# FFN-in of a hybrid layer by a block scheme of seven products, with weight sums partly by accumulating DMAs

## The chip, the core and the metric

The kernel runs on one core of one Trainium2 chip. The metric is the device time of one execution in microseconds (us): 807.37 us, the median of three runs (807.11 to 808.28).

## What is computed

One layer of a decoder trunk: 512 tokens, model width 1024, all in float32. A mixer of three parts (short convolution, stick-breaking attention, a chunked scan) is merged by gates and projected by w_o; then comes a gated FFN of width 2816. Each sub-layer is scaled and shifted by rows that a conditioning vector c gives through mod_w.

```python
mod = jax.nn.silu(c) @ mod_w + mod_b
shift1, scale1, gate1, shift2, scale2, gate2 = split(mod, 6)
...
merged = sigmoid(gl_a) * y_a + sigmoid(gl_b) * y_b + sigmoid(gl_c) * y_c
mix_out = merged @ w_o
x = x + gate1 * rms_norm(mix_out, g_post_mix)

h2 = rms_norm(x, g_pre_ffn) * (1 + scale2) + shift2
gt, up = jnp.split(h2 @ w_ffn_in, 2, axis=-1)
f = (jax.nn.silu(gt) * up) @ w_ffn_out
return x + gate2 * rms_norm(f, g_post_ffn)
```

## The kernel before

**Products in parts.** Each float32 operand is split into a high part (a cast to float32r) and a low part (the rest); a product is three matmuls into one PSUM bank: high by high, high by low, low by high (mm3, L150 to L153). split (L146 to L148) makes the parts: ACT casts (L147), DVE subtracts (L148).

**Weights.** SP loads each weight chunk into one of three raw buffers of 128x2048 (raw_tile, L74). split_piece takes 1024 columns of it and makes a piece, whi and wlo, in one of four buffers each. piece() (L212) hands out the next piece and lets the splits run three pieces ahead (LOOK). All chunks stand in one list in the order of use, the columns of mod_w for the modulation rows between them.

**Order.** The start is scheduled by hand (L316). From there a scheduler puts the instructions of PE, DVE, ACT and POOL in an order and each engine runs its own list in order. PSUM has eight banks that are handed out in turn.

**Modulation rows.** mods_in_turn (L894) is a side job that is pumped along beside the attention, the gates and FFN-out. A step covers 256 columns: mod_acc multiplies and adds the eight row groups of a mod_w chunk on DVE (L230 once, L232 seven times), L906 adds the bias, which POOL loads (L903), and two matmuls with ones spread the row over the partitions. Some steps lie beside the attention, whose own chain on DVE and POOL is sb_e (L591), the mask (L573, POOL), sb_hi (L596) and sb_lo (L597), and on PE the matmul pz (L625).

**Merge and w_o.** The three gated branches are multiplied and added on DVE (L954 and the next lines) and split. w_o runs in two pairs of 128-token blocks; after each block x1_chain (L975) norms, adds the residual and makes two tiles xm (L996), and h2_tiles (L1000) transposes them (L1004) and splits the result into h2h and h2l (L1007, L1008).

**FFN-in.** 22 column blocks of 128 for the gate and 22 for the up half, k = 1024 in eight steps, three matmuls each. The first two blocks of each half run on tokens 0 to 255 first, because the last two xm are not ready then, and on tokens 256 to 511 after; the other 20 pairs run 512 tokens wide (ffn_mm, L1030; L1040 to L1056). Behind each pair, ACT makes the sigmoid and DVE two products (L1060, L1061), and split makes fh and fl.

**FFN-out.** For each half of the output columns, all blocks of f by w_ffn_out, 512 wide, into a bank for each 128 tokens (L1070 to L1121).

Of the kernel before, what the change touches and what calls it, by code (L numbers as in the profile page):

```python
# [7 lines left out]
F32 = mybir.dt.float32  # L8
# [24 lines left out]
def hybrid_block(ctx: ExitStack, tc, x, c, mod_w, mod_b, g_pre_mix, g_post_mix, g_pre_ffn,  # L33
# [112 lines left out]
    def split(hi, lo, src):  # L146
        act.copy(hi, src)  # L147
        vec.tensor_tensor(lo, src, hi.bitcast(F32), ALU.subtract)  # L148
# [26 lines left out]
    def load_chunk():  # L175
        kind, groups, ncol, npc = chunks[at["dma"]]
        at["dma"] += 1
        got = []
        for parts in groups:
            raw = raw_tile()[:, 0:KD * 256 if kind != "cols" else KD * ncol]  # L180
            raw = raw.rearrange("p (k n) -> p k n", n=ncol)
            for k0, nk, src in parts:
                pat = "(p k) n -> p k n" if kind == "mod" else "(k p) n -> p k n"
                nc.sync.dma_start(raw[:, k0:k0 + nk, :], src.rearrange(pat, k=nk))
            got.append(raw)
        if kind == "mod":
            raws.append(got[0])
        for j in range(npc):
            for raw in got:
                pieces.append((kind, raw, ncol, j))  # L190

    def split_piece():
        while at["split"] >= len(pieces):
            load_chunk()
        kind, raw, ncol, j = pieces[at["split"]]
        n = {"cols": P, "v": 264, "rows": ncol}[kind]
        nk = {"cols": KD, "v": 2, "rows": 1024 // n}[kind]
# [14 lines left out]
    def piece():  # L212

        i = at["use"]
        at["use"] += 1
        while at["split"] < min(i + LOOK, n_pieces):
            with tc.high_priority() if at["split"] < 5 else nullcontext():
                split_piece()
        return pieces[i]

    def mod_chunk():
# [6 lines left out]
    def mod_acc(acc, mw):  # L228

        vec.tensor_scalar(acc, mw[:, 0], sc8[:, 0:1], None, op0=ALU.mult)  # L230
        for r in range(1, KD):
            vec.scalar_tensor_tensor(acc, mw[:, r], sc8[:, r:r + 1], acc, op0=ALU.mult,  # L232
                                     op1=ALU.add)

# [217 lines left out]

    def w_mod(part, q4):
        n0 = part * D + q4 * 256
        chunks.append(("mod", [[(0, KD, mod_w[:, n0:n0 + 256])]], 256, 0))
# [21 lines left out]
    for _ in range(2):  # L477
        for kp in range(4):
            w_rows(w_o, 2 * kp, 2, slice(0, D), D)
    for mp in range(MF // 2):  # L480
        chunks.append(("cols", [[(0, KD, w_ffn_in[:, o + mp * 256:o + (mp + 1) * 256])]
                                for o in (0, FFN)], 256, 2))
    for hf in range(2):
        for k0 in range(0, MF, 4):
            w_rows(w_ffn_out, k0, min(4, MF - k0), half(hf), 512)
            if hf == 0 and k0 // 4 < 4:
                w_mod(5, k0 // 4)
    n_pieces = sum(ch[3] * len(ch[1]) for ch in chunks)
# [404 lines left out]

    def mods_in_turn(steps, rest):  # L894

        def sums(part, q4):
            dsts, gain, plus = rows_of[part]
            n0 = part * D + q4 * 256
            if gain is not None and q4 % 2 == 0:
                nc.gpsimd.dma_start(dsts[q4 // 2],  # L900
                                    gain[0, q4 * 256:q4 * 256 + 512].partition_broadcast(P))
            brow = sm.tile([1, 256], F32, tag="brow", name="brow", bufs=2)
            nc.gpsimd.dma_start(brow, mod_b[n0:n0 + 256].unsqueeze(0))  # L903
            acc = sm.tile([P, 256], F32, tag="macc", name="macc2")
            mod_acc(acc, mod_chunk())
            vec.tensor_tensor(acc[0:1, :], acc[0:1, :], brow, ALU.add)  # L906
            am = sm.tile([P, 2, 256], FR, tag="mah", name="mah", bufs=1)
            split(am[:, 0, :], am[:, 1, :], acc)
            return am

        def row(part, q4, am):
            dsts, gain, plus = rows_of[part]
            dst = dsts[q4 // 2][:, (q4 % 2) * 256:(q4 % 2) * 256 + 256]
            pm = bank("pmr")
            pe.matmul(pm[:, 0:256], onesr, am[:, 0, :], start=True, stop=False)
            pe.matmul(pm[:, 0:256], onesr, am[:, 1, :], start=False, stop=True)
            if gain is None:
                act.copy(dst, pm[:, 0:256])
            else:
                vec.scalar_tensor_tensor(dst, pm[:, 0:256], plus, dst, op0=ALU.add,  # L920
                                         op1=ALU.mult)
        last = None
        for n, st_ in enumerate(steps):
            if last is not None:
                row(*last)
            last = st_ + (sums(*st_),)
            yield
            if rest and n % 2:
                yield
        yield  # L930
        row(*last)


    mh, ml = [], []
    sides.append(mods_in_turn(mods, True))
    for mp in range(4):
# [6 lines left out]
        for j in range(2):  # L943
# [3 lines left out]
            for b, (k0, nk, bh, bl) in enumerate(((0, 2, yah, yal), (2, 2, ybh, ybl),  # L947
# [6 lines left out]
                vec.tensor_tensor(gt, gt, pb, ALU.mult)  # L954
                if b:
                    vec.tensor_tensor(gt, gt, acc, ALU.add)
                acc = gt
            mh.append(t2("mh", FR))
            ml.append(t2("ml", FR))
            split(mh[m], ml[m], acc)  # L960
        gts = nxt


    h2h = gp.tile([P, KD, T], FR, tag="h_hi", name="h2h")
    h2l = gp.tile([P, KD, T], FR, tag="h_lo", name="h2l")
    x1 = gp.tile([P, NTB, D], F32, tag="x16", name="x1")
# [32 lines left out]

    def h2_tiles(tb, xms):  # L1000
        for q in range(2):
            pt = bank("pt2")
            for j in range(4):
                pe.transpose(pt[:, blk(j)], xms[q][:, blk(j)], ident)  # L1004
            p3 = pt.rearrange("p (k t) -> p k t", k=4)
            dst = slice(4 * q, 4 * q + 4)
            act.copy(h2h[:, dst, blk(tb)], p3)  # L1007
            vec.tensor_tensor(h2l[:, dst, blk(tb)], p3, h2h[:, dst, blk(tb)].bitcast(F32),  # L1008
                              ALU.subtract)

# [18 lines left out]

    def ffn_mm(pt, w, ts, first, last):  # L1030
        for k in range(KD):
            mm3(pt[:, ts], w[0][:, k, :], w[1][:, k, :], h2h[:, k, ts], h2l[:, k, ts], k == 0,
                k == KD - 1)

    lo_t, hi_t, all_t = slice(0, 256), slice(256, 512), slice(0, 512)
    pf = {}
    fw = {}
    for i in range(4):
        pf[i], fw[i] = bank("pf"), piece()
        ffn_mm(pf[i], fw[i], lo_t, True, False)  # L1040
        if i == 2:
            h2_tiles(*todo.pop(0))
    h2_tiles(*todo.pop(0))
    ma.close()
    fp = ctx.enter_context(tc.tile_pool(name="fp", bufs=1))
    fq = ctx.enter_context(tc.tile_pool(name="fq", bufs=2))
    fh = fp.tile([P, MF, T], FR, name="fh")
    fl = fp.tile([P, MF, T], FR, name="fl")
    for i in range(4):
        ffn_mm(pf[i], fw[i], hi_t, False, True)  # L1050
    for m in range(MF):
        if m < 2:
            pg, pu = pf[2 * m], pf[2 * m + 1]
        else:
            pg, pu = bank("pfg"), bank("pfu")
            for pt in (pg, pu):  # L1056
                ffn_mm(pt, piece(), all_t, True, True)
        f = fq.tile([P, T], F32, tag="f", name="f")
        sigm(f, pg)
        vec.tensor_tensor(f, f, pg, ALU.mult)  # L1060
        vec.tensor_tensor(f, f, pu, ALU.mult)  # L1061
        split(fh[:, m, :], fl[:, m, :], f)

# [6 lines left out]
    def fo_mm(o, tb, w, k0, cs):  # L1070
        for k in range(2):
            mm3(o[:, cs], fh[:, k0 + k, blk(tb)], fl[:, k0 + k, blk(tb)], w[0][:, k, cs],
                w[1][:, k, cs], k0 + k == 0, k0 + k == MF - 1)

    NPF = MF // 2
    for hf in range(2):
# [5 lines left out]
        for i in range(NPF - LATE):  # L1082
            w = piece()
            for tb, acc, cs in groups:
                fo_mm(acc, tb, w, 2 * i, cs)
            if hf == 0:
                if i == 0:
                    sides.append(mods_in_turn([(5, q4) for q4 in range(4)], False))
                pump()
        for i in range(NPF - LATE, NPF):  # L1090
            ws[i] = piece()
        for tb, acc, cs in groups:
            for i in range(NPF - LATE, NPF):
# [55 lines left out]
```

## Time and profile before

| what | value |
|---|---|
| median of three runs | 807.37 us (807.11 to 808.28) |
| the profiled execution | 807.41 us |
| its span in the profile | 805.7 us |
| FFN-in on PE (first start to the first of FFN-out) | 429.2 to 675.7 us |
| FFN-out on PE | from 675.7 us |
| mean granted clock | 0.997 |

The profile is one execution. Its span goes from the first to the last instruction; the execution's own time has 1.7 us more around it. PE is the matmul engine and PEld its weight loads, DVE, ACT, POOL and SP are the others, and a q behind a name means its DMA queue. L with a number is a line of the kernel. In rows of the timeline stand the start, the duration, the engine and line, the operation with output and input, shapes, and in brackets the idle time before it and what ended it.

### The profile page before, as it was taken

Reading aid. Unit: us, or ns where it says so; the run is one execution under the profiler, and the core shown is the slowest. Engines: PE = TensorE matmul, PEld = TensorE weight load, DVE = VectorE, ACT = ScalarE, POOL = GpSimd, SP = SyncE. Lnnn points to the kernel's source line nnn. Section 1 sums busy time; section 2 is a strip of 40 time slices with the busy share of each in tenths; the row PEclk is TensorE's granted clock in tenths of the full one; section 3 lists DMA queues with packets and bytes.
Section 4 is the critical chain, followed back from the end, with each engine's and each line's share of the span. In section 5 each row is a group of like instructions: output and inputs, shape, how many; then the busy total and the mean of one; then the engine's idle time right before and its main releaser. Section 6 shows DMA issues by size and latency. Waiting matters only on the chain.

```text
span 805.7 us, 9651 instructions
## 1 busy us (share of the span) xinstructions
PE 775.2 (96%) x3677; PEld 634.2 (79%) x3677; DVE 495.5 (62%) x783; ACT 373.2 (46%) x625; POOL 122.5 (15%) x169
## 2 busy tenths in 40 slices
PE   3899999999899999999999999999999999999997
PEld 2679887767578888888878988888888888888886
DVE  5999968568967968748498544334344357423214
ACT  5566544565667445463465534434334433213112
POOL 4453412345421000000033000000000000000000
PEclk9999999999999999999999999999999999999999
DMA  9981441120534566452754322322333345532102
GB/s 281 297 258 58 130 131 53 53 85 31 184 121 154 187 201 206 129 173 101 262 169 145 102 84 78 103 81 79 102 105 104 105 148 195 170 115 96 35 1 105
DMA packets 96959, 105.07 MB, mean 130 GB/s; under 512 B 3276, under 2 KB 86272, under 8 KB 96912
## 3 DMA queue, kind: packets, MB, share of 16 engines
q1 hardware_dynamic: 94320, 99.62, 38.6%
q0 software_dynamic: 1824, 3.75, 1.6%
q10 hardware_dynamic: 768, 1.07, 0.4%
q8 instruction: 29, 0.48, 0.2%
q14 instruction: 18, 0.15, 0.1%
HBM read 102.33 MB, written 2.10 MB: 130 GB/s over the span
## 4 chain that ended last, share of the span: by engine, by line
PE 83%; DVE 11%; DMA 2%; issue 2%; ACT 1%; POOL 1%; DVEq 0%; POOLq 0%
PE pgt L151 5%; PE pgt L153 5%; PE pgt L152 5%; PE pfg L152 5%; PE pfu L152 5%; PE pfu L151 5%; PE pfg L151 5%; PE pfu L153 4%; PE pfg L153 4%; PE pfo L152 4%; PE pfo L153 4%; PE pfo L151 4%; DVE smacc L254 2%; PE pbr L151 2%; PE pbr L152 2%; PE pbr L153 2%
## 5 line engine op out<-in xcount | busy, mean ns | idle before, releaser
L147 ACT CAST whi<-wraw 128x1024 fp32r<-128x1024 f32 (+1 forms) x133 | 137.7, 1035 | 303.4 <-PE pfg L152 77.5
L148 DVE TENSOR_TENSOR wlo<-wraw,whi 128x1024 fp32r<-128x1024 f32 (+1 forms) x133 | 164.4, 1236 | 152.8 <-ACT whi L147 148.0
L151 PE MATMUL pgt<-hh,whi 128*128 128x512 f32 x192 | 75.7, 394 | 0.0
L153 PE MATMUL pgt<-hh,wlo 128*128 128x512 f32 x192 | 75.4, 393 | 0.0
L152 PE MATMUL pgt<-hl,whi 128*128 128x512 f32 x192 | 75.4, 393 | 0.0
L152 PE MATMUL pfu<-h2l,whi 128*128 128x512 f32 x160 | 63.0, 394 | 0.0
L152 PE MATMUL pfg<-h2l,whi 128*128 128x512 f32 x160 | 63.0, 394 | 0.0
L151 PE MATMUL pfu<-h2h,whi 128*128 128x512 f32 x160 | 62.7, 392 | 0.0
L151 PE MATMUL pfg<-h2h,whi 128*128 128x512 f32 x160 | 62.7, 392 | 0.0
L153 PE MATMUL pfu<-h2h,wlo 128*128 128x512 f32 x160 | 62.1, 388 | 0.0
L153 PE MATMUL pfg<-h2h,wlo 128*128 128x512 f32 x160 | 62.1, 388 | 0.0
L153 PE MATMUL pfo<-whi,fl 128*128 128x512 f32 x154 | 60.9, 395 | 0.0
L152 PE MATMUL pfo<-wlo,fh 128*128 128x512 f32 x154 | 60.9, 395 | 0.0
L151 PE MATMUL pfo<-whi,fh 128*128 128x512 f32 x154 | 60.8, 395 | 0.0
L903 POOL DMA_DIRECT2D brow<-in_mod_b_dram x16 | 8.1, 504 | 332.0 <-DVE macc L906 331.4
L232 DVE SCALAR_TENSOR_TENSOR macc<-wraw,sc,macc 128x256 f32<-128x256 f32 x112 | 55.8, 499 | 3.2
L153 PEld LDWEIGHTS pgt<-hh,wlo 128*128 128x128 f32 x192 | 36.1, 188 | 8.2
L151 PEld LDWEIGHTS pgt<-hh,whi 128*128 128x128 f32 x192 | 36.1, 188 | 7.8 <-issue 0.4
L152 PEld LDWEIGHTS pgt<-hl,whi 128*128 128x128 f32 x192 | 36.1, 188 | 7.5
L1061 DVE TENSOR_TENSOR f<-f,pfu 128x512 f32<-128x512 f32 x20 | 13.8, 688 | 40.3 <-PE pfu L153 40.3
L151 PEld LDWEIGHTS pfu<-h2h,whi 128*128 128x128 f32 x160 | 30.0, 188 | 7.0
L151 PEld LDWEIGHTS pfg<-h2h,whi 128*128 128x128 f32 x160 | 30.0, 188 | 7.0
(360 smaller groups left out, 1701.5 us busy)
## 6 DMA issues: line engine op xcount, KB each, us to landing
wraw<-in_w_ffn_in_dram SPq DMA_DIRECT2D x22, 1024.0 KB, 5.1
wraw<-in_w_in_dram SPq DMA_DIRECT2D x20, 1024.0 KB, 5.3
wraw<-in_mod_w_dram SPq DMA_DIRECT2D x16, 1024.0 KB, 5.4
wraw<-in_w_ffn_out_dram SPq DMA_DIRECT2D x10, 1024.0 KB, 5.0
wraw<-in_mod_w_dram SPq DMA_DIRECT2D x16, 512.0 KB, 6.1
wraw<-in_w_o_dram SPq DMA_DIRECT2D x8, 1024.0 KB, 4.9
xn<-in_x_dram SPq DMA_DIRECT2D x8, 256.0 KB, 5.7
wraw<-in_w_ssm_out_dram SPq DMA_DIRECT2D x4, 512.0 KB, 7.0
```

Source lines behind the costliest of these rows:

```text
L147: act.copy(hi, src)
L148: vec.tensor_tensor(lo, src, hi.bitcast(F32), ALU.subtract)
L151: pe.matmul(o, whi, xhi, start=start, stop=False)
L152: pe.matmul(o, whi, xlo, start=False, stop=False)
L153: pe.matmul(o, wlo, xhi, start=False, stop=stop)
L232: vec.scalar_tensor_tensor(acc, mw[:, r], sc8[:, r:r + 1], acc, op0=ALU.mult, op1=ALU.add)
L254: vec.scalar_tensor_tensor(acc[:, r % 2, :], mw2[:, r], sc8[:, r:r + 1], acc[:, r % 2, :], op0=ALU.mult, op1=ALU.add)
L903: nc.gpsimd.dma_start(brow, mod_b[n0:n0 + 256].unsqueeze(0))
L1061: vec.tensor_tensor(f, f, pu, ALU.mult)
```

## The change

**The scheme.** FFN-in is computed by unit: two column blocks (0 and 1) of both the gate and the up half, so 11 units. The k range is halved, the tokens are halved. In place of eight block products there are seven per unit; each (product, numbered 1 to 7) is 24 matmuls: gate and up, four k steps, three parts, 256 tokens wide. Four take plain weights, and three (5, 6 and 3) take sums of weights. On the other side, products take sums of the token halves.

**Weight sums.** For a unit, wino_load loads 1 MB per column block in two halves with rows of 512 bytes; every fourth goes into a new, fourth raw buffer. DVE adds the two k halves of block 1 (wsum, L262). POOL issues a DMA that adds block 0 into block 1 in SBUF (L263, 512 KB), and, after the splits of pieces 5 and 6, DMAs that add block 0's halves to wsum (L270, 512 KB each). That makes three such adds per unit.

**Activation sums and results.** For the second token half, DVE and ACT make the sums and split them (L1147 to L1168), before product 5. The PSUM results are combined on DVE (L1196 to L1236). The first two units run side by side, with products 1 and 2 on the first token half first. f stays in float32 (f4s); its split is moved into FFN-out (f_split).

**Modulation rows and merge.** A modulation step now covers 512 columns in two chunks of four row groups; the first row is scaled on ACT (L965), the seven others are added on DVE (L967), and the bias is added by an accumulating DMA. The sums of the merge are accumulating DMAs but for the last block (L1014), and a merged block is split one block later.

The diff, cut to its core:

```diff
+    NU = MF // 2
+    WINO = [(u, q) for q in (1, 2, 5, 6, 7, 4, 3) for u in range(2)]
+    WINO += [(u, q) for u in range(2, NU) for q in (5, 1, 4, 6, 7, 2, 3)]
...
+    def wino_load(u, i):
+        at["wino"] = at.get("wino", 0) + 1
+        if at["wino"] % 4:
+            raw = raw_tile()
+        else:
+            raw = late_pool["fx"].tile([P, 2048], F32, tag="raw4", name="wraw", bufs=1)
...
+            nc.sync.dma_start(raw[:, g], w_ffn_in[:, c0:c0 + P].rearrange(
+                "(k p) n -> p k n", k=8))
...
+        if q == 5:
...
+            vec.tensor_tensor(un["s"], un[1][0], un[1][1], ALU.add)
+            nc.gpsimd.dma_start(un[1][0], un[0][0], accum_op=ALU.add)
+        src = {1: (0, 0), 2: (0, 1), 4: (1, 1), 7: (1, 0)}.get(q)
+        src = un[src[0]][src[1]] if src else un["s"]
...
+        split(hi, lo, src)
+        if q in (5, 6):
+            nc.gpsimd.dma_start(un["s"], un[0][q - 5], accum_op=ALU.add)
...
-    mods = [(p_, q4) for p_ in (2, 3, 4) for q4 in range(4)]
+    mods = [(p_, hf, rh) for p_ in (2, 3, 4) for hf in range(2) for rh in range(2)]
...
+            for rh in range(2):
+                mw = mod_chunk()
+                for r in range(4):
+                    c_ = sc8[:, 4 * rh + r:4 * rh + r + 1]
+                    if rh + r == 0:
+                        act.activation(acc, mw[:, r], AF.Copy, scale=c_)
+                    else:
+                        vec.scalar_tensor_tensor(acc, mw[:, r], c_, acc, op0=ALU.mult,
+                                                 op1=ALU.add)
...
+            nc.gpsimd.dma_start(acc[0:1, :], mod_b[n0:n0 + 512].unsqueeze(0), accum_op=ALU.add)
...
+                elif m < 7:
+                    nc.gpsimd.dma_start(acc, gt, accum_op=ALU.add)
...
+                for part, (a_, b_) in enumerate(((hi, xh), (hi, xl), (lo, xh))):
+                    pe.matmul(o[:, cs], a_[:, g, k, :], b_,
+                              start=(start and g + k + part == 0),
+                              stop=(stop and k == 3 and part == 2), skip_group_check=True)
...
+        vec.tensor_tensor(t1_, hbh[:, 0, :, t0].bitcast(F32), p12, ALU.subtract)
+        vec.tensor_tensor(t1_, t1_, hbl[:, 0, :, t0].bitcast(F32), ALU.add)
+        split(hbh[:, 3, :, t0], hbl[:, 3, :, t0], t1_)
...
+    for u in range(2, NU):
+        p5 = bank("pf5")
+        product(5, p5, True, True)
+        pa1, u2 = bank("pfa"), u2_tile()
+        product(1, pa1, True, True)
+        act.copy(u2, pa1)
+        p4 = bank("pf4")
+        product(4, p4, True, True)
+        p6 = bank("pf6")
+        product(6, p6, True, True)
+        vec.tensor_tensor(u2, p6, u2, ALU.add)
+        p7 = bank("pf7")
+        product(7, p7, True, True)
...
+        vec.tensor_tensor(c2[:, 0, :], p7, u2, ALU.add)
+        vec.scalar_tensor_tensor(c2[:, 1, :], p5, -1.0, c2[:, 0, :], op0=ALU.mult,
+                                 op1=ALU.subtract)
+        vec.tensor_tensor(c2[:, 0, :], p4, c2[:, 0, :], ALU.subtract)
+        gated_m1(u, c2)
+        product(2, pa1, False, True)
+        gated_m0(u, pa1, 0)
+        product(3, p5, False, True)
+        vec.tensor_tensor(u2, p5, u2, ALU.add)
+        gated_m0(u, u2, 1)
...
+    with tc.high_priority():
+        f_split(0)
+        f_split(1)
```

**How the order moves.** At the start of FFN-in, DVE before, from the last xm (the tiles that PE transposes) on; wlo are low parts of weights, pt2 the transposed tiles, f the gated result:

```order
L996 SCALAR_TENSOR_TENSOR xm_3880<-xm_3880,st_3868,SH_2233 128x512
L996 SCALAR_TENSOR_TENSOR xm_3886<-xm_3886,st_3868,SH_2234 128x512
L1008 TENSOR_TENSOR h2l_3477<-pt2_4027,h2h_3476 128x4x128
L1008 TENSOR_TENSOR h2l_3477<-pt2_4034,h2h_3476 128x4x128
L148 TENSOR_TENSOR wlo_3957<-wraw_3952,whi_3956 128x1024
L1060 TENSOR_TENSOR f_4146<-f_4146,pf_3893 128x512
```

The same place after, first piece; u2, sg and c2 hold sums of the activations, txh, txl, hbh and hbl their parts:

```order
L1058 SCALAR_TENSOR_TENSOR xm_3765<-xm_3765,st_3753,SH_2233 128x512
L1058 SCALAR_TENSOR_TENSOR xm_3771<-xm_3771,st_3753,SH_2234 128x512
L262 TENSOR_TENSOR wsum_3928<-wraw_3678 128x1024
L1156 TENSOR_TENSOR u2_3938<-hbh_3356,pt2_3866 128x512
L1162 TENSOR_TENSOR u2_3940<-sg_3939,pt2_3866 128x512
L148 TENSOR_TENSOR wlo_3932<-wsum_3928,whi_3931 128x1024
L1157 TENSOR_TENSOR u2_3938<-u2_3938,hbl_3357 128x512
L148 TENSOR_TENSOR txl_3937<-u2_3940,txh_3936 128x4x128
L1160 SCALAR_TENSOR_TENSOR c2_3941<-u2_3938,sg_3939 128x512
L148 TENSOR_TENSOR hbl_3357<-u2_3938,hbh_3356 128x4x128
L1164 TENSOR_TENSOR c2_3941<-hbh_3356,c2_3941 128x512
L148 TENSOR_TENSOR txl_3937<-c2_3941,txh_3936 128x4x128
```

Six rows on (left out here: L1165, hbl, L1156, txl, L1157, L1162), the second piece, up to the weights of product 5 of unit 1:

```order
L1160 SCALAR_TENSOR_TENSOR c2_3962<-u2_3959,sg_3960 128x512
L148 TENSOR_TENSOR hbl_3357<-u2_3959,hbh_3356 128x4x128
L148 TENSOR_TENSOR txl_3937<-u2_3961,txh_3936 128x4x128
L148 TENSOR_TENSOR txl_3937<-c2_3962,txh_3936 128x4x128
L1164 TENSOR_TENSOR c2_3962<-hbh_3356,c2_3962 128x512
L148 TENSOR_TENSOR hbl_3357<-sg_3960,hbh_3356 128x4x128
L1165 TENSOR_TENSOR c2_3962<-c2_3962,hbl_3357 128x512
L262 TENSOR_TENSOR wsum_3998<-wraw_3995 128x1024
L148 TENSOR_TENSOR txl_3937<-c2_3962,txh_3936 128x4x128
L1172 TENSOR_TENSOR f4_3914<-sg_3980,pfa_3778 128x256
L1173 TENSOR_TENSOR f4_3914<-f4_3914,pfa_3778 128x256
L148 TENSOR_TENSOR wlo_4002<-wsum_3998,whi_4001 128x1024
```

Where two subtractions (h2l) followed the last xm, the activation sums and two weight sums with their low parts follow now.

At the start of FFN-out, DVE before; macc2 is a modulation step, the matmuls of FFN-out begin with blocks whose fl lies far ahead of these rows:

```order
L148 TENSOR_TENSOR wlo_5532<-wraw_5529,whi_5531 128x1024
L1060 TENSOR_TENSOR f_5512<-f_5512,pfg_5452 128x512
L1061 TENSOR_TENSOR f_5512<-f_5512,pfu_5453 128x512
L230 TENSOR_SCALAR macc2_5661<-wraw_5662,sc8_132 128x256
L148 TENSOR_TENSOR wlo_5576<-wraw_5529,whi_5575 128x1024
L148 TENSOR_TENSOR fl_4049<-f_5512,fh_4048 128x512
```

After, from the last combination (L1234, which reads product 3) on; fparts with f4_3914 is the first unit's low part of f:

```order
L1234 TENSOR_TENSOR u2_6276<-pf5_6246,u2_6276 128x512
L1173 TENSOR_TENSOR f4_3924<-f4_3924,c2_6395 128x512
L148 TENSOR_TENSOR wlo_6538<-wraw_6497,whi_6537 128x1024
L1172 TENSOR_TENSOR f4_3924<-sg_6435,pfa_6275 128x256
L967 SCALAR_TENSOR_TENSOR macc2_6532<-wraw_6569,sc8_132,macc2_6532 128x512
L1173 TENSOR_TENSOR f4_3924<-f4_3924,pfa_6275 128x256
L967 SCALAR_TENSOR_TENSOR macc2_6532<-wraw_6569,sc8_132,macc2_6532 128x512
L1172 TENSOR_TENSOR f4_3924<-sg_6470,u2_6276 128x256
L967 SCALAR_TENSOR_TENSOR macc2_6532<-wraw_6569,sc8_132,macc2_6532 128x512
L1173 TENSOR_TENSOR f4_3924<-f4_3924,u2_6276 128x256
L148 TENSOR_TENSOR fparts_6481<-f4_3914,fparts_6480 128x1024
```

The low part that FFN-out needs first has moved from the stage before to the end of this list.

More of the change, by code (lines that the diff above doesn't have):

```diff
@@ L892, in hybrid_block, with mods_in_turn, row @@
     rows_of = {2: (G1, g_post_mix, 0.0), 3: (SH, None, 0.0), 4: (SC, g_pre_ffn, 1.0)}
-    def mods_in_turn(steps, rest):
-        def sums(part, q4):
+    def mods_in_turn(steps, rest, parts_):
+        def row(part, hf, am):
             dsts, gain, plus = rows_of[part]
[L898 to L913, printed above, removed]
+            dst = dsts[hf]
@@ L927, in mods_in_turn @@
             yield
-            if rest and n % 2:
+            am = parts_()
+            split(*am, acc)
+            last = (part, hf, am)
+            if rest:
                 yield
@@ L1027, in hybrid_block @@
             todo.append((tb, x1_chain(tb, pos[tb])))
[L1030 to L1042, printed above, removed]
@@ L1043, in hybrid_block @@
-    h2_tiles(*todo.pop(0))
-    ma.close()
[L1045 to L1062, printed above, removed]
+    lo_t, hi_t = slice(0, 256), slice(256, 512)
```

236 lines of the change are left out of this document (193 added, 43 removed).

## The prediction

> **What bounds the kernel now.** I read the page's first part and its chain, then PE's waits by stage, then the busy time of each engine in the FFN-in stage, then single rows of DVE and PE where the change puts work in PE's way. The page's engine row and chain row:
>
> ```profile
> PE 775.2 (96%) x3677; PEld 634.2 (79%) x3677; DVE 495.5 (62%) x783; ACT 373.2 (46%) x625; POOL 122.5 (15%) x169
> PE 83%; DVE 11%; DMA 2%; issue 2%; ACT 1%; POOL 1%; DVEq 0%; POOLq 0%
> ```
>
> PE is busy for 96% of the span and carries 83% of the chain. Where it waits at all from 180 us on, the waits view names three places (total, times, longest):
>
> ```profile
> PE pz L625 <- DVE sb_hi L596: 1.9, 1, 1.9
> PE pz L625 <- DVE sb_lo L597: 1.2, 1, 1.2
> PE pt L1004 <- DVE xm L996: 2.5, 2, 1.4
> ```
>
> The first two lie in the stick-breaking attention, the third at the border of w_o and FFN-in. Inside FFN-in nothing waits; the windows view from 480 to 680 us (busy PE, PEld, DVE, ACT, POOL, clock, DMA share, GB/s):
>
> ```profile
> 480.00:680.00 200.00, 200.00 (x875) 164.02 (x874) 89.37 (x113) 80.81 (x109) 2.13 (x4) 1.00 0.33 108
> ```
>
> So a matmul less there is time off the end, if DVE (45% busy), ACT (40%) and the DMAs can feed the shorter stage, and if PE starts and ends it as promptly as before.
>
> **Term 1, matmuls.** PE's timeline, the first and the last of 72 matmuls of 256 columns in a row, then the first and last starts of the 512-wide FFN-in and of FFN-out by tile:
>
> ```profile
> 429.22 0.28 PE L151 MATMUL pf<-h2h,whi 128*128 128x256 f32 x1
> 437.58 0.28 PE L153 MATMUL pf<-h2h,wlo 128*128 128x256 f32 x1
> L151 PE MATMUL pfg<-h2h,whi x160: 392/392/392, 456.0 to 669.5; 128*128 128x512 f32 x160
> L151 PE MATMUL pfo<-whi,fh x154: 392/394/398, 675.7 to 794.9; 128*128 128x512 f32 x154
> ```
>
> A 256-wide matmul takes 8.36/71 = 0.1177 us; 960 wide ones took 675.7 - 456.0 = 219.7 us, 0.2288 each. FFN-in was 192 x 0.1177 + 219.7 = 242.3 us. The change issues 11 units x 7 products x 24 = 1848 matmuls of 256 columns: 217.6 us. Term: -24.7. Only seven eighths of the multiplications are left, and the narrow form gives 3% of that back. The Trainium skill, "TensorE: Matmul & The Clock Gate", Part 1: The HAM clock gate, has back-to-back matmuls at N/2.4 GHz plus about 2.5 ns. By it they would be 109 and 216 ns (estimate from that page) and the term -26.3; the rows are 6 to 8% slower, and the rows decide.
>
> **Term 2, the start of FFN-in (seam 1).** The four products on the first token half come first as before. Before, PE then needed the last xm, eight transposes and one copy. DVE's xm and PE around it:
>
> ```profile
> 442.17 1.41 DVE L996 SCALAR_TENSOR_TENSOR xm<-xm,st,SH 128x512 f32<-128x512 f32 x2
> 441.28 0.28 PE L153 MATMUL pf<-h2h,wlo 128*128 128x256 f32 x1
> 442.98 1.32 PE L1004 MATMUL pt<-ident,xm 128*128 128x128 f32 x8 [1.42 <-DVE xm L996]
> 444.31 0.74 PE L151 MATMUL pf<-h2h,whi 128*128 128x256 f32 x4
> 445.04 0.39 PE L152 MATMUL pf<-h2l,whi 128*128 128x256 f32 x1
> ```
>
> Four matmuls before 445.04 at full pace is 444.6, PE's restart free of stalls. Now the order has 18 DVE instructions after those xm before the last low part that product 5 reads (L148 hbl<-u2_3959, itself the eighteenth): two of 1024 columns, two scalar_tensor_tensor of 512, fourteen others of 512. Their start-to-start from DVE's timeline, with two 256-wide rows for later:
>
> ```profile
> 413.02 1.22 DVE L148 TENSOR_TENSOR wlo<-wraw,whi 128x1024 fp32r<-128x1024 f32 x1
> 414.15 0.69 DVE L988 TENSOR_TENSOR x<-x,t2k 128x512 f32<-128x512 f32 x1
> 414.75 0.69 DVE L1008 TENSOR_TENSOR h2l<-pt,h2h 128x512 fp32r<-128x512 f32 x1
> 415.36 0.74 DVE L986 SCALAR_TENSOR_TENSOR t2k<-pwo,st,G 128x512 f32<-128x512 f32 x1
> 416.01 0.68 DVE L1008 TENSOR_TENSOR h2l<-pt,h2h 128x512 fp32r<-128x512 f32 x1
> 205.81 0.42 DVE L779 TENSOR_TENSOR ce<-ce,xs 128x256 f32<-128x256 f32 x1
> 206.14 0.69 DVE L815 TENSOR_TENSOR ys<-ys,sgz 128x512 f32<-128x512 f32 x1
> ```
>
> That is 1.13 for 1024 columns, 0.605 for 512, 0.65 for scalar_tensor_tensor, 0.33 for 256. So 2 x 1.13 + 2 x 0.65 + 14 x 0.605 = 12.0; DVE is free of xm at 443.5, PE restarts at T = 455.5, 10.9 later than 444.6. Nothing else is ready for PE then. Behind T, ten more DVE instructions up to wlo_4002, which product 5 of unit 1 reads (six of 512 columns, two of 256, two of 1024: 6 x 0.605 + 2 x 0.33 + 2 x 1.13), end at T + 6.5, while product 5 of unit 0 lasts 2.8, so PE waits again. Then the POOL add of unit 1 (L270) goes out, and product 6 of unit 1 needs it landed, cast and subtracted. No accumulating DMA is in this trace. The nearest rows: POOL's own loads, a 1 KB one, and the weights (KB each, median us to landing); with them the group rows of the cast and of four POOL issues:
>
> ```profile
> x<-in_x_dram POOLq DMA_DIRECT2D x4, 512.0 KB, 5.2
> SC<-in_g_pre_ffn_dram POOLq DMA_DIRECT2D x2, 256.0 KB, 7.1
> G<-in_g_post_mix_dram POOLq DMA_DIRECT2D x2, 256.0 KB, 3.5
> wraw<-in_w_ffn_in_dram SPq DMA_DIRECT2D x22, 1024.0 KB, 5.1
> wraw<-in_mod_w_dram SPq DMA_DIRECT2D x16, 512.0 KB, 6.1
> wraw<-in_mod_w_dram SPq DMA_DIRECT2D x16, 1024.0 KB, 5.4
> L147 ACT CAST whi<-wraw 128x1024 fp32r<-128x1024 f32 (+1 forms) x133 | 137.7, 1035 | 303.4 <-PE pfg L152 77.5
> L968 POOL DMA_DIRECT2D x<-in_x_dram x4 | 2.1, 538 | 37.8 <-PE pbr L153 37.8
> ```
>
> I take A = 5.2 us for an add of 512 KB, the POOL row of the same size, and keep 3.5 and 7.1 as ends. Product 6 of unit 1 can start at T + 6.5 + 0.5 (issue) + 5.2 + 1.04 + 1.13 = T + 14.4; without waits it would start three products (8.5) after T. That is 5.9 more, and 10.9 + 5.9 = 16.8. Term: +16.8 (15.1 to 18.7).
>
> By the Trainium skill, "Collectives: The Full Stack", The bandwidth ceiling: the fold count and why AG ≠ RS ≠ AR, an add in a DMA reads two sources for one write, so twice the reading of a copy. An estimate by that page is an add that lasts as much longer than a plain load as 512 KB more would, 6 to 7 us, and a forecast some 1.5 us higher; no run shown has such a transfer, and the sum stays with the rows.
>
> **Term 3, the start of FFN-out (seam 2).** Before, fl of the last block was not needed first, and no wait is listed there. Now the first split of f (f_split(0)) stands on DVE behind all of the last unit: after PE's end of product 3, L1234, L1173 of 512, a wlo, four 256-wide, three L967, and the split itself: 0.6 + 0.6 + 1.13 + 4 x 0.33 + 3 x 0.65 + 1.13 = 6.7. Two matmuls (0.46) need only the high part, so PE stands for 6.3. After such idling the clock is low; windows around the attention's two waits (clock is the third number from the end):
>
> ```profile
> 212.00:214.00 2.00, 0.50 (x1) 0.19 (x1) 1.81 (x4) 0.34 (x1) 0.49 (x2) 1.00 0.00 0
> 214.00:216.00 2.00, 1.44 (x5) 0.91 (x7) 2.00 (x6) 0.00 (x0) 0.00 (x0) 0.60 0.00 0
> 216.00:218.00 2.00, 2.00 (x14) 1.36 (x16) 1.67 (x3) 1.97 (x4) 1.30 (x2) 0.55 0.78 250
> 218.00:220.00 2.00, 2.00 (x16) 1.39 (x13) 1.08 (x2) 0.81 (x3) 1.76 (x2) 1.00 1.07 362
> ```
>
> Four us at 0.575 after 3.1 us of waiting lose 1.7. Term: +6.3 + 1.7 = +8.0 (6.3 to 9). In seam 1 the same loss falls into the wait until T + 6.5 and costs nothing.
>
> **Term 4, the attention's waits.** DVE's rows ahead of them, and SP's two loads of modulation weights:
>
> ```profile
> 206.74 1.12 DVE L230 TENSOR_SCALAR macc<-wraw,sc 128x256 f32<-128x256 f32 x1
> 207.89 3.21 DVE L232 SCALAR_TENSOR_TENSOR macc<-wraw,sc,macc 128x256 f32<-128x256 f32 x5
> 212.28 0.49 DVE L596 CAST sb_hi<-sb_e 128x512 fp32r<-128x512 f32 x1 [0.19 <-POOL sb_e L573]
> 212.69 1.21 DVE L148 TENSOR_TENSOR wlo<-wraw,whi 128x1024 fp32r<-128x1024 f32 x1
> 213.82 0.68 DVE L597 TENSOR_TENSOR sb_lo<-sb_e,sb_hi 128x512 fp32r<-128x512 f32 x1
> 177.73 22.03 SPq L184 DMA_DIRECT2D wraw<-in_mod_w_dram  x2
> ```
>
> The new steps put 1.3 us of L967 and a wlo there in place of 4.3 us of L230 and L232, and sb_lo follows sb_hi at once. If that were all, both waits (3.1) and most of the clock loss (1.7) would go. But L967 now also stands in front of the sb_hi of the step before, and reads the second half chunk, whose load could go out only at 177.73 + 22.03 = 199.8. With 5.4 us it lands at 205.2, up to 1.3 sooner as the first half needs less of DVE. From there 0.65 + 0.33 + 0.65 + 0.6 to that sb_lo, 5.3 of work up to the next sb_e, then 0.6, 0.7 for the mask, 0.33 and 0.6 end sb_lo at 213.6 to 214.9, where 214.5 was. I take -0.3, and half of the clock loss, -0.9. Term: -1.2 (-4.5 to +4).
>
> **What costs nothing, and its cover.** Steady units last 168 x 0.1177 = 19.8 us. DVE has 8 x 1.13 + 6 x 0.6 + 0.65 + 4 x 0.33 = 14.6 in each, so it keeps up. The adds and loads form a loop: in an even unit, a load L, two POOL issues, an add, cast and subtract, an issue and an add (2A + L + 3.7), since POOL has the next unit's L263 ahead of L270; in an odd one two loads, two issues and an add (A + 2L + 1). Together 3(A + L) + 4.7 must stay under 39.6, so A + L under 11.6. With 5.2 and 5.1 it does. The accumulating adds of the merge (L1014), the wider modulation rows and the later f splits lie beside matmul work of 5 us and more per step; I put them at 0, at most +2.
>
> **Sum.** The profiled execution took 807.41 us (its span 805.7 and 1.7 around it), the median of the runs 807.37, so no shift between them. -24.7 + 16.8 + 8.0 - 1.2 = -1.1: 806.3 us, which is no change: 0.2%, about what a measurement of this kernel can tell from none, is 1.6 us.
>
> **Rivals.** *Adds land late in the loop (slower).* For: 256 KB on POOL's queue took 7.1 where other loads ran, and the new weight loads come in 512-byte rows, as the 512 KB loads of 6.1 us do. Against: DMA share is 0.33 in this stage. With A = 7.1 and L = 5.1 each pair of units runs 1.8 late, five pairs 9; the split ahead of product 6 has 2.7 of slack, and seam 1 takes 1.9 more: +8, 814. With L = 6.1 it is +23, 829. I set 820. It decides from A + L of about 12. Chance 0.20.
>
> *The seams cost less (faster).* If the half chunk lands in time, term 4 is -4.5 (3.3 less); if adds land in 3.7 us, seam 1 loses 1.5 less; if no clock loss follows seam 2, 1.7 less. All three: 799.8. For: the adds stay within SBUF. Against: DVE's order is fixed and its counts are certain. Chance 0.25.
>
> *The half chunk lands late*, as at 6.1 us or behind other loads, and holds both attention steps: term 4 at +4, 811.5. For: DVE stands in order behind it. Against: 1 MB loads of that kind took 5.4. Chance 0.09.
>
> That the stage isn't shortened at all I rule out: the order shows all 1848 matmuls at 256 columns.
>
> **Chances.** The forecast has 0.46, with its own range 798 to 813 (0.18 faster, 0.14 within 0.2%, 0.14 slower). The seams' rival adds 0.25 to faster; the late adds 0.19 to slower and 0.01 to same; the half chunk 0.06 to slower, 0.01 to same, 0.02 to faster. Faster 0.45, same 0.16, slower 0.39. The range runs from 797 to 826.
>
> **What would show it.** Right: PE's waits in FFN-in name DVE hbl or hbh for 10 to 12 us at the start, wlo twice after, and fparts for about 6 at FFN-out's start; between them PE is busy throughout at 0.118 us each, and POOL's 512 KB adds land in about 5 us. Wrong: PE waits on whi or wlo in every second unit (late adds), a gap before FFN-out under 3 us, or a seam 1 under 12 us.

## The result and the profile after

| | before | after |
|---|---|---|
| median | 807.29 us (807.11 to 808.28, 4 runs) | 860.66 us (858.72 to 863.31, 4 runs) |
| ratio, 95% interval | | 1.0661 (1.0628 to 1.0693) |
| profiled execution's span | 805.7 us | 860.0 us |
| FFN-in on PE, first start to the first of FFN-out | 429.2 to 675.7: 246.5 us | 427.8 to 726.1: 298.3 us |
| from there to the end of the span | 130.0 us | 133.9 us |

The change made the kernel 6.6% slower; the forecast was no change, 797 to 826 us. The ends of the stage are read from the first and last starts by tile (the products 1 and 2 open FFN-in, pfo is FFN-out):

```profile
L1110 PE MATMUL pfa<-hbh,whi x176: 276/279/385, 427.8 to 712.5; 128*128 128x256 f32 x176
L151 PE MATMUL pfo<-whi,fparts x154: 392/394/796, 726.1 to 849.1; 128*128 128x512 f32 x154
```

Up to FFN-in the kernel is 1.4 us ahead, in FFN-in it loses 51.8, in FFN-out 3.9: together the 54.3 us by which the span grew. The page's engine row and chain row, in place of 96% and 83% for PE:

```profile
PE 771.6 (90%) x4357; PEld 664.5 (77%) x4357; DVE 555.4 (65%) x796; ACT 425.6 (49%) x698; POOL 174.0 (20%) x208
PE 64%; DVE 14%; DMA 14%; issue 3%; ACT 2%; POOL 1%; SPq 1%; DVEq 0%; POOLq 0%
```

PE still carries most of the chain, but DMA has gone from 2% to 14%. The rows of PE's waits that bear on this (total, times, longest):

```profile
PE pf L1110 <- DVE c L1227: 33.7, 7, 8.9
PE pf L1110 <- ACT hbh L147: 10.3, 1, 10.3
PE pfo L151 <- ACT fparts L147: 5.2, 1, 5.2
PE pf L1110 <- DVE c L1205: 3.6, 1, 3.6
PE pf L1110 <- ACT whi L147: 3.4, 5, 1.5
PE pz L670 <- DVE sb_hi L641: 0.6, 1, 0.6
PE pz L670 <- DVE sb_lo L642: 0.2, 1, 0.2
```

The second and third are the two seams, the last two what is left of the attention's waits. The first is new and the largest: L1227 is the combination on DVE that reads product 5's bank before product 3 may add to it. The fourth, L1205, is the same combination in the first two units. The long waits for L1227 come in every second unit; PE's timeline at three of them:

```profile
569.59 0.58 PE L1110 MATMUL pf<-hbh,whi 128*128 128x256 f32 x1 [7.95 <-DVE c L1227]
620.88 0.58 PE L1110 MATMUL pf<-hbh,whi 128*128 128x256 f32 x1 [8.85 <-DVE c L1227]
671.85 0.58 PE L1110 MATMUL pf<-hbh,whi 128*128 128x256 f32 x1 [7.94 <-DVE c L1227]
```

The stalls are 51 us apart, where two units of matmuls would take 39.6. The chain of waits between two of them, the long pieces in order of time:

```profile
542.76 7.12 DMA wsum<-wraw
...
552.58 6.16 DMA wsum<-wraw
...
559.22 6.64 DMA wraw<-in_w_ffn_in_dram
...
567.12 0.68 DVE c L1226
567.80 1.13 DVE wlo L148
568.94 0.61 DVE c L1227
569.59 7.18 PE pf L1110 x47
576.77 2.83 PE pfa L1110 x24
579.60 8.48 PE pf L1110 x72
588.08 2.72 PE pfa L1110 x23
590.83 1.05 ACT whi L147
592.10 0.73 POOL wraw L263
592.83 7.20 DMA wsum<-wraw
```

From 542.76 to 592.83 is one turn of 50.1 us: an add (7.1), the cast, the subtraction and the issue (2.7), the second add (6.2), a load that waited for the buffer that this add read (7.1 with its issue), DVE (3.7), then a whole unit of PE (21.2). Its end lets a cast on ACT go, behind which POOL issues the next block add; the first add of the next even unit stands behind that in POOL's order (2.0). One row of DVE ties the load into it: the weight sum of the next unit stands in front of this unit's combinations and waits for its weights.

```profile
565.98 1.22 DVE L262 TENSOR_TENSOR wsum<-wraw 128x1024 f32<-128x1024 f32 x1 [3.13 <-DMA wraw<-in_w_ffn_in_dram]
```

The DMA view (KB each, median us to landing) has the adds, and the loads in their two halves of 512 KB:

```profile
wraw<-in_w_ffn_in_dram SPq DMA_DIRECT2D x44, 512.0 KB, 6.7
wsum<-wraw POOLq DMA_DIRECT2D x22, 512.0 KB, 6.2
wraw<-wraw POOLq DMA_DIRECT2D x11, 512.0 KB, 5.1
```

Waiting costs more than its own length. The 298.3 us of the stage are 217.6 of matmuls at full pace, 59.4 of waits, 2.5 of transposes, and some 19 us that are left. Most of these are time in which PE runs at a lower granted clock behind its stalls: PE's busy time by what the clock lacked of 1.00, added up over windows of 1 us, is 15.6 us. Windows right behind the wait at the start of FFN-out (clock third from the end):

```profile
726.00:728.00 2.00, 1.40 (x3) 0.68 (x4) 2.00 (x4) 2.00 (x4) 0.83 (x1) 0.50 0.87 281
728.00:730.00 2.00, 2.00 (x5) 1.61 (x6) 2.00 (x3) 1.80 (x2) 0.00 (x0) 0.50 0.95 310
730.00:732.00 2.00, 2.00 (x6) 1.52 (x6) 2.00 (x3) 1.93 (x2) 0.00 (x0) 0.50 0.89 333
```

### The profile page after: what moved, and what is told of

It is laid out like the page before. It is cut to its first block, busy times and chain, and to the rows that moved or that the text cites. A ratio compares the mean times of both kernels' runs of the same rounds, so it can differ in the third digit from the quotient of the medians.

```text
span 860.0 us, 11349 instructions
## 1 busy us (share of the span) xinstructions
PE 771.6 (90%) x4357; PEld 664.5 (77%) x4357; DVE 555.4 (65%) x796; ACT 425.6 (49%) x698; POOL 174.0 (20%) x208
## 4 chain that ended last, share of the span: by engine, by line
PE 64%; DVE 14%; DMA 14%; issue 3%; ACT 2%; POOL 1%; SPq 1%; DVEq 0%; POOLq 0%
PE pf L1110 9%; DMA wsum<-wraw 7%; PE pgt L151 5%; PE pgt L152 5%; PE pgt L153 5%; PE pfo L153 4%; PE pfo L152 4%; PE pfo L151 4%; DMA wraw<-in_w_ffn_in_dram 4%; DVE wlo L148 3%; DMA wraw<-in_mod_w_dram 3%; PE pfa L1110 3%; DVE smacc L299 2%; PE pbr L152 2%; PE pbr L153 2%
## 5 line engine op out<-in xcount | busy, mean ns | idle before, releaser
L1110 PE MATMUL pf<-hbh,whi 128*128 128x256 f32 x176 | 56.5, 321 | 48.8 <-DVE c L1227 33.7
L1110 PE MATMUL pf<-txh,whi 128*128 128x256 f32 x264 | 74.7, 283 | 2.2 <-ACT whi L147 2.2
L1110 PE MATMUL pf<-txl,whi 128*128 128x256 f32 x264 | 74.4, 282 | 0.0
L1110 PE MATMUL pf<-txh,wlo 128*128 128x256 f32 x264 | 74.4, 283 | 0.0
L151 PE MATMUL pfo<-whi,fparts 128*128 128x512 f32 x154 | 62.2, 404 | 5.2 <-ACT fparts L147 5.2
L153 PE MATMUL pfo<-whi,fparts 128*128 128x512 f32 x154 | 62.0, 402 | 0.5 <-DVE fparts L148 0.5
L152 PE MATMUL pfo<-wlo,fparts 128*128 128x512 f32 x154 | 62.0, 402 | 0.0
L1110 PE MATMUL pf<-hbh,wlo 128*128 128x256 f32 x176 | 54.4, 311 | 1.2 <-DVE wlo L148 1.2
L1110 PE MATMUL pf<-hbl,whi 128*128 128x256 f32 x176 | 54.7, 311 | 0.6 <-DVE hbl L148 0.6
L270 POOL DMA_DIRECT2D wsum<-wraw x22 | 28.0, 1276 | 127.1 <-DVE wlo L148 117.4
L1110 PEld LDWEIGHTS pf<-txh,whi 128*128 128x128 f32 x264 | 50.2, 190 | 2.9 <-ACT whi L147 2.9
L967 DVE SCALAR_TENSOR_TENSOR macc<-wraw,sc,macc 128x512 f32<-128x512 f32 x56 | 44.2, 788 | 11.7 <-ACT macc L965 7.5
L1110 PEld LDWEIGHTS pf<-txl,whi 128*128 128x128 f32 x264 | 50.3, 190 | 0.0
```

The lines of the kernel that those rows point to most:

```text
L151: pe.matmul(o, whi, xhi, start=start, stop=False)
L152: pe.matmul(o, whi, xlo, start=False, stop=False)
L153: pe.matmul(o, wlo, xhi, start=False, stop=stop)
L270: nc.gpsimd.dma_start(un["s"], un[0][q - 5], accum_op=ALU.add)
L967: vec.scalar_tensor_tensor(acc, mw[:, r], c_, acc, op0=ALU.mult, op1=ALU.add)
L1110: pe.matmul(o[:, cs], a_[:, g, k, :], b_, start=(start and g + k + part == 0), stop=(stop and k == 3 and part == 2), skip_group_check=True)
```

## The experiments

The theory after the result: every second unit hangs on the chain above, through DVE's order. The rivals: DVE has too much work (1); the DMAs' traffic as such (2); an adding DMA costs much more than a copy (3). Where no interval is given, the time is that of one run; the kernel before took 806.6 to 807.8 us beside them. Repeated runs of one of these kernels lie 2.8 to 4.6 us apart, so a difference of some 4 us between single runs shows little by itself.

**No adds.**

```diff
-            nc.gpsimd.dma_start(un[1][0], un[0][0], accum_op=ALU.add)
...
-            nc.gpsimd.dma_start(un["s"], un[0][q - 5], accum_op=ALU.add)
```

> The 33 accumulating DMAs of the weights are left out, so products 3, 6 and 7 use wrong weights and the output is not the layer's. Theory (every second unit hangs on a chain of two adds and a load that stands in front of the combinations on DVE): the 33.7 us of waits for L1227 and some 10 us of low clock behind them go; 806 to 820 us. Rival 1 (DVE has too much work in a unit): nothing of DVE's work goes, 845 us or more. Rival 2 (the DMAs' traffic): also 806 to 820, told apart by the other runs.

Measured: 816.1 us. Some 44 us hang on the adds, and rival 1 is out. The wait for L1227 shrinks from 33.7 to 6.3 us.

**Copies in their place.**

```diff
-            nc.gpsimd.dma_start(un[1][0], un[0][0], accum_op=ALU.add)
+            nc.gpsimd.dma_start(un[1][0], un[0][0])
...
-            nc.gpsimd.dma_start(un["s"], un[0][q - 5], accum_op=ALU.add)
+            nc.gpsimd.dma_start(un["s"], un[0][q - 5])
```

> The same 33 DMAs of 512 KB as plain copies from buffer to buffer, so the sums are wrong. Theory: only their landing time counts, and it changes little (5 to 6 us), 845 to 860 us. Rival 3 (an adding DMA costs much more than a copy because it reads twice): copies land in 4 us or less, each pair of units is shorter by 4 us or more, 835 us or less.

Measured: 823.9 us. The DMA view of this run:

```profile
wraw<-in_w_ffn_in_dram SPq DMA_DIRECT2D x44, 512.0 KB, 5.4
wsum<-wraw POOLq DMA_DIRECT2D x22, 512.0 KB, 3.4
wraw<-wraw POOLq DMA_DIRECT2D x11, 512.0 KB, 3.1
```

Rival 3 holds: between the same buffers and in the same order, an add lands after 6.2 and 5.1 us where a copy takes 3.4 and 3.1, and the weights beside it land 1.3 us later. The Trainium skill, "Collectives: The Full Stack", The bandwidth ceiling: the fold count and why AG ≠ RS ≠ AR, says that an add reads two sources; these runs agree with it in size (1.8 and 1.6 times), but they don't show what in the add takes the time. My own expectation, that the landing would change little, was wrong. With as many DMAs of the same size in the same queue and order, 36.7 of the 44 us are gone.

**The combinations first.** wsum is multiplied by a flag of one that DVE writes behind the combinations of the unit before:

```diff
-            vec.tensor_tensor(un["s"], un[1][0], un[1][1], ALU.add)
+            if "c2" in late_pool:
...
+                vec.tensor_scalar(fl, late_pool["c2"][:, 1, 0:1], 0.0, 1.0, op0=ALU.mult,
+                                  op1=ALU.add)
+                vec.scalar_tensor_tensor(un["s"], un[1][0], fl, un[1][1], op0=ALU.mult,
+                                         op1=ALU.add)
```

> All adds stay, and the output is right. The weight sum on DVE (L262) multiplies by a flag of one that is written after the combinations of the unit before, so it can no longer stand in front of them, and POOL's block add moves behind both adds of the unit before. Theory: the 8 to 9 us stalls in every second unit go, each unit may wait 1 to 2 us for product 5's weights instead; 815 to 835 us. Rival 2 (traffic) and rival 1 (DVE): as much traffic and slightly more DVE work, 858 us or more.

Measured: 856.4 us, 4.3 less, where 815 to 835 us were expected. My theory fell: DVE's order is where the chain shows, not its cause. POOL's timeline of this run (here L270 is the block add and L277 the adds into wsum):

```profile
543.29 1.20 POOL L277 DMA_DIRECT2D wsum<-wraw  x1 [2.15 <-DVE wlo L148]
551.03 1.20 POOL L277 DMA_DIRECT2D wsum<-wraw  x1 [6.53 <-DVE wlo L148]
564.18 1.20 POOL L270 DMA_DIRECT2D wraw<-wraw  x1 [11.95 <-DVE wsum L266]
567.53 1.20 POOL L277 DMA_DIRECT2D wsum<-wraw  x1 [2.16 <-DVE wlo L148]
```

The first adds of two units in a row are 24.2 us apart: every unit is late now, where before a turn of two units took 50. A turn is two adds in series with the cast and subtraction between, then the split behind them, the combinations and sigmoids, which stand behind the waiting casts on ACT and DVE, and the next split. So the new theory is that the two adds of a unit in series are the chain, whatever the order around them.

**Which adds?** First the block add alone by DVE:

```diff
-            nc.gpsimd.dma_start(un[1][0], un[0][0], accum_op=ALU.add)
+            vec.tensor_tensor(un[1][0], un[1][0], un[0][0], ALU.add)
```

> The add of block 0 into block 1 (L263) is done by DVE, the 22 adds into wsum stay DMAs. Theory: POOL's queue no longer holds the add behind product 5's split of an even unit until the next unit's buffer is loaded; the stalls of 8 to 9 us fall to 3 or less, 815 to 830 us. Rival 1 (DVE): 11 us more of DVE work make it slower, 865 to 870. Rival 2 (traffic): a third of the adds is gone, 845 us.

Measured: 3433.3 us. This says nothing of the edit: PE's group row for the gates, hundreds of us ahead of it, has 1698 ns where before had 394.

```profile
L151 PE MATMUL pgt<-hh,whi 128*128 128x512 f32 x192 | 326.0, 1698 | 0.0
```

What made PE so slow in that execution is open. The same kernel once more:

> The block add (L263) by DVE once more, since in the run before PE was four times slower from its first stage on, in code that the edit does not touch. Theory as it stands now (an adding DMA lands after 5 to 6 us, two of them stand in series in a unit, in queues that the combinations share): the two adds into wsum stay, so much of the loss stays, 830 to 850 us. Theory of the queue order alone: 815 to 830.

Measured: 854.3 us. 11 of 33 adds less gain 6 us, not the 10 or more that I had expected. Now the other way round, the two adds into wsum by DVE and the block add as a DMA:

```diff
-            nc.gpsimd.dma_start(un["s"], un[0][q - 5], accum_op=ALU.add)
+            vec.tensor_tensor(un["s"], un["s"], un[0][q - 5], ALU.add)
```

> The other way round from the block add by DVE: the 22 adds into wsum by DVE, the 11 block adds (L263) stay DMAs; the output is right. Theory (two adds in series between the splits of a unit are the chain, the block add has nothing in series behind it): nearly all of the loss goes, 812 to 820 us. Rival 2 (traffic, each add costs alike, 44 us over 33): 826 to 830 us.

Measured: 817.6 us, 43 less. PE's wait for L1227 falls from 33.7 us to

```profile
PE pf L1110 <- DVE c L1227: 5.0, 4, 2.4
```

The 11 block adds land after 5.0 us as they did (5.1) and cost little: 43 us for the 22 adds into wsum are 2.0 each, while the block adds are worth 6 us in the run before and 4 in the next, some 0.4 to 0.6 each. Rival 2, by which all adds cost alike, is out.

**All sums by DVE.** Both edits together.

> All three weight sums of a unit by DVE, no adding DMA in FFN-in; the output is right. Theory (the adds' landing time is what costs): as without adds, and 3.4 us of DVE work more in a unit of 19.8, so 814 to 826 us. Rival 1 (DVE is the limit, 18.0 of 19.8 us): 830 us or more.

Measured: 813.2 us. DVE does 3.4 us more in each unit, and what PE still waits for weights and combinations in FFN-in is 4.0 us in all. The two long waits that are left, 12.5 and 6.6 us, are the seams.

**Seam 1, the order.** All sums by DVE, and the activation sums that product 5 doesn't read stand behind it, as do the first gated results (the core of the edit):

```diff
     both(5)
+    sums(2)
+    sums(3)
```

> As all sums by DVE, and the activation sums that product 5 doesn't read stand behind it in the program. My step on seam 1 (DVE's instructions between the last xm and product 5 are what PE waits for): 9 of them in place of 18, 7.0 us in place of 12.0, so 4 to 7 us under the run with all sums by DVE. Rival (the wait is for weights): no difference within 1 us.

Measured: 813.7 us, no gain. PE's timeline of this run:

```profile
444.73 0.58 PE L1110 MATMUL pf<-hbh,whi 128*128 128x256 f32 x1 [3.96 <-ACT whi L147]
447.13 0.58 PE L1110 MATMUL pf<-hbh,wlo 128*128 128x256 f32 x1 [1.60 <-DVE wlo L148]
465.22 1.01 PE L1110 MATMUL pf<-txh,whi 128*128 128x256 f32 x3 [9.79 <-ACT txh L147]
```

Product 5 starts at 444.7, where it started at 453.4 in the run with all sums by DVE, and the first matmul of product 6 (txh) at 465.2, where it was at 460.7. The wait has moved from one to the other, since DVE is busy without a gap from 440 to 460 (its busy time is the third figure of the window):

```profile
440.00:460.00 20.00, 9.86 (x54) 9.02 (x52) 20.00 (x24) 8.44 (x10) 0.00 (x0) 0.74 0.19 53
```

Seam 1 is DVE's work up to product 6, in the order in which it stands.

**Seam 2.** In addition the first split of f in the last unit, in the fourth load buffer:

```diff
+        if u == NU - 1:
+            f0 = late_pool["p0"].tile([P, 4, T], FR, tag="raw4", name="fparts", bufs=1)
...
+            split(fhs[0], fls[0], f4s[0])
```

> As the run before, and the split of the first unit of f is made ahead of the last unit's end, in the buffer of the fourth weight load. My step on seam 2 (PE waits some 6 us for this split and then loses clock): 6 to 9 us under the run before. Rival (something else is late next, such as the weights of FFN-out): 3 us or less.

Measured: 807.0 us, 6.8 less. FFN-out's first matmul no longer waits; one wait of 2.4 us remains at 679 us, for the second unit's split.

**POOL's own adds.** In addition the block add and the last add of the first two units by POOL as an engine:

```diff
-            vec.tensor_tensor(un[1][0], un[1][0], un[0][0], ALU.add)
+            (pool if u < 2 else vec).tensor_tensor(un[1][0], un[1][0], un[0][0], ALU.add)
```

> As the run with both seams, and in the first two units POOL does the block add and the last add as instructions of its own, not DMAs. The run before showed that DVE is busy without a gap from 440 to 470 us, so that seam 1 is a sum of DVE's work up to product 6, not a matter of which product comes first: 4 x 1.13 = 4.5 us of it less, 801 to 804 us. Rival (the activation sums' order alone): no change within 1 us; or POOL slows DVE's reads and nothing is gained.

Measured: 810.4 us, where 801 to 804 were expected; nothing is gained. POOL's first add, and DVE's rows beside it and behind it:

```profile
444.27 3.27 POOL L263 TENSOR_TENSOR wraw<-wraw 128x1024 f32<-128x1024 f32 x1 [5.76 <-DMA wraw<-in_w_ffn_in_dram]
```

```profile
445.26 3.37 DVE L148 TENSOR_TENSOR wlo<-wsum,whi 128x1024 fp32r<-128x1024 f32 x1
448.56 1.21 DVE L262 TENSOR_TENSOR wsum<-wraw 128x1024 f32<-128x1024 f32 x1
```

DVE's subtraction takes 3.37 us, where its like take 1.22, and ends 1.1 us after POOL's add. One DVE instruction at each of the four POOL adds is longer by 2.1 to 2.2 us, together more than the 4.5 us taken off DVE. The Trainium skill, "SBUF — State Buffer", Who interferes with whom, has it that a DVE instruction with two SBUF inputs contends with a GpSimd one that reads SBUF; the run agrees.

**By need.** POOL's adds as before, and the activation sums in the order of products 6, 7, then 4 and 3:

```diff
-    sums(2)
-    sums(3)
+    for stage in (sums6, sums7, sums4):
+        stage(2)
+        stage(3)
```

> As the run before, with the activation sums in the order of need (all that product 6 reads, then 7, then 4 and 3). Theory (PE waits for DVE's work up to the first product that lacks its input): product 6 can start some 6 us sooner, the rest lies beside products 6 and 7; 793 to 800 us. Rival: the total of DVE's work until product 3 sets the end, no more than 1 us.

Measured: 805.7 us, 4.7 less, about as much as repeated runs differ, and not the 793 to 800 expected.

**Modulation later.** In addition the last modulation steps one chunk later:

```diff
-            if hf == 0 and k0 // 4 < 4:
-                w_mod(5, k0 // 8, k0 // 4 % 2)
+            if hf == 0 and 0 < k0 // 4 < 5:
+                w_mod(5, (k0 // 4 - 1) // 2, (k0 // 4 - 1) % 2)
...
-                if i == 0:
+                if i == 2:
```

> As the run before, with the modulation steps of FFN-out one chunk later, so that fewer of them stand on DVE in front of the second unit's split of f: PE's last wait of 2.4 us at the start of FFN-out and the low clock behind it fall, 1 to 3 us less than the run before. Rival: the wait is for the split itself, no change.

Measured: 811.5 us, ratio to before 1.0041 (1.0028 to 1.0054): slower, against the expectation. DVE's timeline shows a modulation step in front of the last product of f that waits 3.43 us for its load; on SP a load of w_ffn_out (669.0) now goes out ahead of that load (672.1):

```profile
680.65 0.75 DVE L968 SCALAR_TENSOR_TENSOR macc<-wraw,sc,macc 128x512 f32<-128x512 f32 x1 [3.43 <-DMA wraw<-in_mod_w_dram]
```

**By need without POOL.** The order by need, all weight sums by DVE again, modulation as in the change.

> The activation sums in the order of need, all weight sums by DVE, the first split of f early, no POOL adds. Theory (POOL's adds held DVE's instructions up, three or four of them by 2.1 us each; the order by need is worth the 4.7 us that it gave beside POOL): 801 to 804 us, that is 3 to 6 us under the kernel before. Rival (only the total of DVE's work counts): 806 to 807, as the run with both seams.

Measured: 803.3 us, ratio to before 0.9944 (0.9925 to 0.9962). This lies within the 801 to 804 expected, so the order by need is worth something without POOL.

**Adding DMAs where nothing waits.** In addition the block add and the last add of the first two units as adding DMAs:

```diff
+            if u < 2:
+                nc.gpsimd.dma_start(un[1][0], un[0][0], accum_op=ALU.add)
+            else:
+                vec.tensor_tensor(un[1][0], un[1][0], un[0][0], ALU.add)
...
+            if u < 2 and q == 6:
+                nc.gpsimd.dma_start(un["s"], un[0][1], accum_op=ALU.add)
```

> As the run before, and in the first two units the block add and the last add are adding DMAs, which nothing waits for in series for 10 us or more: 4 x 1.13 = 4.5 us of DVE's work less in seam 1. Theory (seam 1 is DVE's work up to product 6): two of these four adds stand before product 6's inputs on DVE, so 2 to 4.5 us under the run before, 798 to 801 us. Rival (their landing comes late for products 7 and 3): no gain or slower.

Measured: 796.4 us, ratio to before 0.9855 (0.9832 to 0.9879), 1.4% faster than the kernel before and below the 798 to 801 expected. All its waits of FFN-in over 1 us, in place of 33.7 and 10.3:

```profile
PE pf L1116 <- ACT whi L147: 4.0, 1, 4.0
PE pfo L151 <- ACT fparts L147: 2.3, 1, 2.3
PE pt L1073 <- DVE xm L1064: 2.1, 2, 1.1
PE pf L1116 <- DVE c L1257: 1.8, 4, 0.5
PE pf L1116 <- DVE sg L1179: 1.6, 1, 1.6
PE pf L1116 <- DVE wlo L148: 1.3, 2, 0.9
```

FFN-in lasts from 426.0 to 660.2, 234.2 us against 246.5 before. 4.5 us less of DVE's work gave 6.9 us. Between the two profiles PE's waits in the stage fall by some 3 us, and the granted clock from 460 to 480 us rises from 0.83 to 1.00; the gain is not taken apart further.

## Why the prediction was wrong, point by point

**Right: the matmuls (-24.7).** Between stalls they run at 0.118 us each, and with most stalls out of the way half of their gain is seen in the last experiment (234.2 us against 246.5).

**Right in place and size: seam 1 (+16.8).** Product 5 runs freely from 454.5, 11.3 us after the 443.2 at which it would start with this run's lead of 1.4 (10.9 forecast). Product 6 of unit 1 begins at 468.1 and runs freely from 469.3, that is T + 14.8 (T + 14.4 forecast). Not in the term are a second spell of low clock (0.50 to 0.56 from 470.3 to 473.7) and the wait of 3.6 us for L1205 at 494.9; the latter belongs to the adds, as it is 0.7 us with the two adds into wsum on DVE. What I had also not seen is that the total of DVE's work up to product 6 sets it: the run that only reordered gained nothing, the ones that reordered by need and took DVE's work away did.

**Right: seam 2 (+8.0).** PE waits 5.2 and 0.5 us, 5.7 (6.3 forecast), and the low clock costs some 3 us (1.7 forecast): 0.50 for 6 us, not 0.575 for 4. Moving the split gave 6.8 us back with 2.4 of waiting left.

**Right in sign, but too small: the attention (-1.2).** FFN-in began 1.4 us sooner, which is this close by luck: the start of this profile took 1.5 us longer (the last matmul into xbc, ahead of the attention, is at 59.5 in place of 58.0). From there to FFN-in it is 368.3 us in place of 371.2, so 2.9 were gained. Of 3.1 us of waiting 2.3 went, where I had counted on 0.3.

**Wrong: the steady units (0).** The step that failed is "What costs nothing, and its cover": that the adds and loads form a loop which holds as long as A + L stays under 11.6, and that the split ahead of product 6 has 2.7 us of slack. The rival of late adds (chance 0.20) named the right place and the wrong price, 814 to 829; its sign, PE waiting on whi or wlo in every second unit, did not show: PE waited there for the combination. Two things were off:
- The loop. I had closed it over loads, adds, their issues and the one cast and subtraction between two adds, as if the other splits, the combinations and PE could slide. They stand in ACT's and DVE's lists in order, so a cast that waits for an add holds the combinations behind it, and PE with them; a whole unit of PE is inside the turn of 50.1 us. With my own A and L (5.2, 5.2 and 5.1 in place of 7.1, 6.2 and 6.6) that turn would still be some 45.7, six over two units.
- The sizes. A was 5.1 to 6.2 and 7.1 where two overlapped, L 6.6 to 6.7. I took A from a load of the same size; adds of this size take 1.6 to 1.8 times a copy between the same buffers, and the loads beside them got 1.3 us slower. With the measured medians (6.2 and 6.7) my own loop gives 43.4 us for two units, 3.8 over the 39.6 of the matmuls, where 51 were measured: the sizes alone are about a third of the excess.

Both turns, 45.7 and 43.4, are worked out, not run.

The price in the sum: 860.7 less the 806.3 forecast is 54 us; taking the two wsum adds off the DMAs alone gives 43 of them back, taking all adds off gives 47, with DVE paying for the sums. The rest of some 7 us, 813.2 against 806.3, is not taken apart into single terms.

## What to carry to other kernels

A transfer in series between two steps of a pipeline is priced as its landing time plus everything that stands behind the waiting instruction on its engine, and the loop has to be closed over the engines' lists, the critical engine's included, before it can be called hidden. Ask of each add not how much it moves but what waits for it within ten microseconds: the same kind of DMA cost 43 us in one place, some 5 in another, and gained time in a third. A seam in which one engine is busy without a gap is shortened by work taken off it, or by doing first what the next product needs; moving work from in front of the first waiter to right behind it only moved the wait.

## What the runs showed of the hardware

- An adding DMA of 512 KB from SBUF to SBUF landed after 5.1 to 6.2 us, a copy after 3.1 to 3.4 (medians); POOL was busy 1.20 us with the issue of an add and 0.72 with that of a copy.
- PE ran at a granted clock of 0.50 behind its waits: for 6 us behind the one of 5.2 (726 to 732 us), for some 6.5 behind the one of 10.3 (453.3 to about 460), for some 3 to 4 behind the three of 8 to 9 in the steady units.
- One DVE instruction at each of four POOL adds of 128x1024 lasted 2.1 to 2.2 us longer than its like (3.37 against 1.22 for 1024 columns).
- One execution had PE's 512-wide matmuls for the gates at 1698 ns in place of 394, with 1.00 as the granted clock on record; its cause is open.
